# Reordering an encoder layer's expert stage: where the permutation is made, which experts come last, and what stands at the end

## The chip, the cores and the metric

The kernel runs on one core of a Trainium2 chip. The core has TensorE (PE, the matrix engine; its weight loads are listed apart as PEld), VectorE (DVE), ScalarE (ACT), GpSimd (POOL) and SyncE (SP), each with its own instruction queue, and 16 DMA engines that move data between the chip's memory (DRAM here) and the on-chip buffers (SBUF; PSUM receives what TensorE computes, in banks of 128x512 float32). The metric is the device time of one execution in microseconds (us).

## The reference

One layer of an encoder over 256 tokens of width 1024: a normalisation, three token mixers side by side, gates, an output projection, a second normalisation, and then a mixture of 32 experts with a last normalisation. The change touches only the last part:

```python
logits = xf @ w_router + b_router              # (256, 32)
top_val, top_idx = lax.top_k(logits, 4)        # four experts for each token
gates = softmax(top_val)
# for each expert e with its tokens:
u = x[toks] @ w1[e] + b1[e]                    # w1[e]: 1024 x 2048
glu, lin = split(u); glu = min(glu, 7); lin = clip(lin, -7, 7)
y = (glu * sigmoid(1.702 * glu) * (lin + 1)) @ w2[e] + b2[e]    # w2[e]: 1024 x 1024
out[toks] += y * gate
h = LN(alpha * h + out, ln2_g, ln2_b)          # alpha = 2 ** 0.25
```

Everything is float32. The weights of all 32 experts (12 MiB each, 384 MiB in all) are read once.

## The kernel before

The first 280 us or so (the trunk) compute the mixers, the second normalisation and the router. There the experts are ranked by their load; rank 0 is always expert 0, rank 1 is the most loaded of the others, rank 31 the least loaded. A rank has room for 128 tokens (ranks 0 to 5), 64 (6 to 19) or 32 (20 to 31). Ranks are put together to **units** of 128 token slots: one rank of 128, a pair of 64, or four of 32. `UNITS` is the order in which the 16 units run. The code behind it, under `tc.If(flag > 0)`, is a fallback for overfull experts; it reads `acc_out` and is skipped here.

**A unit.** `gather` picks the unit's tokens out of `h` with a 0/1 matrix `P` (made by `slots`), into `XT`. `up(u, side)` multiplies by w1: eight steps k, in each one 1 MiB block of w1 for each of the unit's ranks, four 128x512 products (into four `u` banks) for each rank. Products of a pair or of four ranks use 64 or 32 columns of the array each and run side by side. After each step, `used("w1", u, k)` gives the step's block buffers back, and `next(side)` records one piece of other work between this step's products and the next. When the loop is over, the sums are copied out, and the rest of `side` is recorded in one go (`for _ in side: pass`). `gated(u)` turns `U[u]` by TensorE transposes, adds the bias `b1` and computes the activation in two halves f. `down(u, side)` multiplies by w2 in four steps k, in each one 1 MiB block for each rank, with its own side work. `combine(u, t)` scatters a unit's result with `PC[u]` (made by `weigh`) and VectorE adds it to `acc_out`. The order is up(0), then up(u) and down(u-1) for u = 1 to 15, then `closing`, down(15) and `end`. `closing` starts four PSUM sums `acc` with `acc_out` and the last but one unit's result; `end` adds the last unit's, normalises, and stores.

**Side work before.** Beside up(0) stands `opening()`: the sorted list of ranks `pii`, which the loads of ranks 8 to 23 need (`ahead["all"]`), the token positions in rank order, the biases `b1` in rank order (16 small products and two copies by ScalarE), and gather(1). Beside up(1) stand gated(0), `gates()`, `begin` (which starts `acc_out`, with b2 read by a DMA on ScalarE's queue), weigh(0), weigh(1), slots(2), gather(2) and weigh(2). Beside down(14) stand gated(15) and `rows2`, which reads the last norm's gain and bias (`norms`) by a DMA on ScalarE's queue and spreads them over 128 partitions by eight small products.

**What sets the order.** From the trunk's last products on, PE, ACT, DVE and SP run in the order in which the code records them; nothing is rearranged. The weight blocks are read by SP (`pump`, L237) in the order of their use, except that w2 of unit 0 comes before w1 of unit 1. There are 19 buffers of 1 MiB (`RING`); one of them serves once, and the other 18 go round: a block can be read when the block that had its buffer has been used. A block's buffer is given back by the PE product that read it last.

**At the end.** `end` takes statistics of the four sums with VectorE, and works on one quarter with ScalarE and GpSimd, on the others with VectorE (`centre`, `spread`). `S.copy(acc_out[...], acc[...])` writes the four sums back for the fallback. `put` stores the quarters, four by SP and one by ScalarE's queue.

Of the kernel before, what the change touches and what calls it, by code (L numbers as in the profile page):

```python
# [23 lines left out]
T = 256  # L24
# [18 lines left out]


LARGE, MIDDLE = 5, 14
UNITS = [(0,), (28, 29, 30, 31), (1,), (6, 7), (2,), (8, 9), (20, 21, 22, 23), (3,), (10, 11), (4,), (12, 13),
         (24, 25, 26, 27), (5,), (14, 15), (16, 17), (18, 19)]
assert sorted(j for u in UNITS for j in u) == list(range(NE))


# [59 lines left out]
def encoder_layer(ctx, tc, consts, norms, columns, x, positions, w_in, w_gate, rel_bias, conv_w, w_pw2, w_uq, w_ukv,  # L110
# [20 lines left out]
    def bank(pool, name):  # L131
        return pool.tile([128, 512], F32, name=name)
# [853 lines left out]
    R = {}  # L986
# [100 lines left out]

    def opening():

        p = bank(pu, "m")  # L1090
        PE.matmul(p[:1, :NE], cst[:NE, C_P:C_P + 1], R["perm"][:NE], start=True, stop=True)
        R["pii"] = cp.tile([1, NE], I32, name="pii")
        V.tensor_copy(R["pii"], p[:1, :NE])
        ahead["all"] = True
        yield
        R["ps"] = (yield from transposed(R["posm"]))[1]
        slots(1)
        S.activation(cp.tile([128, 1], F32, name="junk"), ones[:, 0:1], AF.Sigmoid)
        yield
        R["b1"] = mp.tile([128, 16, NE], F32, name="b1")  # L1100
        for i in range(2):
            p = bank(pu, "m")
            r = slice(i * NE, (i + 1) * NE)
            for c in range(8):
                f = slice(c // 2 * 256 + c % 2, (c // 2 + 1) * 256, 2)
                PE.matmul(p[:, c * NE:(c + 1) * NE], R["b1r"][r, f], R["perm"][r], start=True, stop=True)

            S.activation(R["b1"][:, 8 * i:8 * i + 8], p[:, :8 * NE].rearrange("p (c e) -> p c e", c=8), AF.Identity,
                         bias=ones[:, 0:1] if i else 0.0)
            yield  # L1110
        yield from gather(1)

    def transposed(src):

# [112 lines left out]
    def up(u, side):  # L1227

        js = UNITS[u]
        n = 128 // len(js)  # L1230
        banks = {cb: pu.tile([128, 512], F32, name="u", bufs=4) for cb in (0, 2, 1, 3)}
        for k in range(8):
            for cb in (0, 2, 1, 3):
                for i, j in enumerate(js):
                    PE.matmul(banks[cb][i * n:(i + 1) * n], XT[u][:, k, i * n:(i + 1) * n],  # L1235
                              block["w1", j, k][:, 0, cb * 512:(cb + 1) * 512], start=(k == 0), stop=(k == 7),
                              skip_group_check=True)
            used("w1", u, k)
            next(side, None)
        us = U[u] = mp.tile([128, 2048], F32, name="us")  # L1240
        for cb, copy in ((0, S.copy), (2, V.tensor_copy), (1, S.copy), (3, V.tensor_copy)):
            copy(us[:, cb * 512:(cb + 1) * 512], banks[cb])  # L1242
        for _ in side:
            pass
# [48 lines left out]
    def beside_up(u):  # L1293

        if u == 1:
            yield
            yield from gated(0)
            yield from gates()
            for t in range(2):
                begin(t)  # L1300
                yield
            yield from weigh(0)
            yield from weigh(1)
        if u + 1 < n_units:
            slots(u + 1)
        yield
        for t in range(2):
            if u > 1:
                combine(u - 2, t)
                yield  # L1310
        if u + 1 < n_units:
            yield from gather(u + 1)
            yield from weigh(u + 1)

    def beside_down(u):

        yield
        if u + 1 < n_units:
            yield from gated(u + 1)
        if u + 2 == n_units:  # L1320
            yield from rows2()

    def experts():
        up(0, opening())
# [8 lines left out]

    def rows2():

        nf = mp.tile([128, T], F32, name="gp")[:8]
        nc.scalar.dma_start(out=nf, in_=norms[8:12].rearrange("r (i n) -> (r i) n", i=2))
        yield
        L["n"] = Norm(cp)
        v = R["slots"].rearrange("p (r i n) -> p r i n", r=4, i=2)  # L1340
        for r in range(4):
            p = bank(pu, "m").rearrange("p (i n) -> p i n", i=2)
            for i in range(2):
                PE.matmul(p[:, i], ident[:8, 2 * r + i:2 * r + i + 1].to_broadcast([8, 128]), nf, start=True, stop=True)
            S.copy(v[:, r], p)
        L["n"].gb = [[R["slots"][:, (2 * i + c) * 512:(2 * i + c + 1) * 512] for i in range(2)] for c in range(2)]
# [11 lines left out]
    def end(u):  # L1358
# [31 lines left out]
        V.tensor_scalar(n2.v[:, 0], n2.mv[:, :, 1], 1e-5, None, op0=OP.add)  # L1390
        centre(0, 1)
        rsqrt(n2.v[:, 1], n2.v[:, 0], n2.v[:, 2])
        for c in range(2):
            S.copy(acc_out[:, 0, cols(c)], acc[0, c])
        S.activation(o0, o0, AF.Copy, scale=n2.v[:, 1, 0:1])
        G_.tensor_add(o0, o0, n2.gb[0][1])
        for c in range(2):
            S.copy(acc_out[:, 1, cols(c)], acc[1, c])
        centre(1, 0)
        spread(0, 1)  # L1400
        centre(1, 1)
# [5 lines left out]
        put(1, 0)  # L1407
        for q in range(2):
            put(1, 1, slice(q * 256, q * 256 + 256))


    warm = tp.tile([128, 1], F32, name="warm")
# [237 lines left out]
```

## Time and profile before

| | |
|---|---|
| median of 3 runs | 1275.05 us (1273.71 to 1275.6) |
| profiled execution | 1275.57 us, of which the profile's span is 1273.7 us |
| PE busy | 1183.7 us, 93% of the span |
| VectorE, ScalarE, GpSimd busy | 412.5, 261.0 and 118.8 us |
| DMA | 449.35 MB, mean 353 GB/s |
| mean granted TensorE clock | 0.97 of full speed |

[...] A busy PE is not a PE at its peak: products are counted as busy for as long as they are in the pipeline, and those that run side by side count once. Each matrix product of float32 appears as two records in the trace, so a step of one rank, four products, is "x8", and a step of four ranks, 16 products, is "x32".

### The profile page before, as it was taken

How to read it: one execution, taken by the hardware profiler on the slowest of the kernel's cores; microseconds unless marked ns; L12 is line 12 of the kernel's file. 1: busy time of each engine (PE TensorE's matmuls, PEld its weight loads, DVE VectorE, ACT ScalarE, POOL GpSimd, SP SyncE). 2: the span in 40 equal slices, each digit the busy share in tenths (PEclk: the TensorE clock that was granted, in tenths of full speed). 3: DMA queues.
4: the chain of work that ended last, by engine and by line, in shares of the span. 5: the costliest groups of instructions: out<-in, count | busy, mean ns of one | idle time of the engine just before them, and what ended most of it. 6: DMA issues, size and time to landing. Idle time of an engine off the chain costs nothing.

```text
span 1273.7 us, 15502 instructions
## 1 busy us (share of the span) xinstructions
PE 1183.7 (93%) x6015; PEld 627.8 (49%) x6015; DVE 412.5 (32%) x705; ACT 261.0 (20%) x486; POOL 118.8 (9%) x164
## 2 busy tenths in 40 slices
PE   8998998999878999999979989999978989999786
PEld 6998988975315534534324424543322523434241
DVE  6568998850203131221202121221201221212012
ACT  5785785521101000010001000010100000100011
POOL 7441752002000000000000000000000000000000
PEclk9999999989988999999999999999998999999978
DMA  8636444599899799999999999999999999999970
GB/s 276 208 133 205 152 131 159 166 374 406 338 421 422 279 398 421 421 421 421 421 421 420 422 421 422 421 422 421 420 422 420 422 420 422 420 422 420 422 324 35
DMA packets 78727, 449.35 MB, mean 353 GB/s; under 512 B 7697, under 2 KB 9346, under 8 KB 29498
## 3 DMA queue, kind: packets, MB, share of 16 engines
q1 hardware_dynamic: 76266, 442.83, 86.2%
q0 software_dynamic: 1648, 4.15, 1.1%
q10 hardware_dynamic: 736, 1.34, 0.3%
q8 instruction: 49, 0.80, 0.3%
q14 instruction: 28, 0.23, 0.0%
HBM read 446.67 MB, written 1.09 MB: 352 GB/s over the span
## 4 chain that ended last, share of the span: by engine, by line
PE 53%; DMA 37%; DVE 8%; issue 1%; ACT 1%; SPq 0%; DVEq 0%; ACTq 0%
PE u L1235 21%; DMA more<-in_w_dram 15%; DMA hi<-in_w_dram 12%; PE y L1282 10%; PE mm L357 9%; DMA raw<-in_w_dram 5%; PE m L1180 4%; DMA klo<-in_w_dram 3%; DVE c L756 3%; PE mm L349 3%; DVE lo L274 2%; PE m L1223 2%; PE u L1259 1%; DMA lo<-in_w_dram 1%; DMA pts<-in_columns_dram 1%
## 5 line engine op out<-in xcount | busy, mean ns | idle before, releaser
L1235 PE MATMUL u<-more,xt 128*64 128x512 f32 (+2 forms) x840 | 246.9, 613 | 12.2 <-DMA more<-in_w_dram 12.1
L1235 PE MATMUL u<-lo,xt 128*32 128x512 f32 (+2 forms) x352 | 151.0, 624 | 4.6 <-DMA lo<-in_w_dram 4.6
L1235 PE MATMUL u<-hi,xt 128*32 128x512 f32 (+2 forms) x320 | 138.5, 621 | 11.2 <-DMA hi<-in_w_dram 11.2
L1235 PEld LDWEIGHTS u<-more,xt 128*64 128x64 f32 (+2 forms) x840 | 79.3, 142 | 130.6 <-issue 100.0
L1235 PE MATMUL u<-raw,xt 128*64 128x512 f32 (+2 forms) x304 | 129.4, 606 | 6.7 <-DMA raw<-in_w_dram 6.7
L1282 PE MATMUL y<-more,xt 128*32 128x512 f32 (+2 forms) x360 | 108.6, 615 | 3.6 <-DMA more<-in_w_dram 3.5
L1225 DVE TENSOR_TENSOR khi<-khi,m 128x512 f32<-128x512 f32 x56 | 38.5, 687 | 195.7 <-PE m L1223 195.7
L357 PE MATMUL mm<-klo,hi 128*128 128x256 f32 (+1 forms) x368 | 100.9, 286 | 0.0
L357 PE MATMUL mm<-khi,hi 128*128 128x256 f32 (+1 forms) x368 | 100.5, 285 | 0.1
L357 PE MATMUL mm<-khi,lo 128*128 128x256 f32 (+1 forms) x368 | 100.2, 285 | 0.0
L274 DVE TENSOR_TENSOR lo<-raw,hi 128x2048 fp32r<-128x2048 f32 (+3 forms) x46 | 86.4, 1892 | 25.1 <-ACT hi L269 25.1
L1372 POOL TENSOR_SCALAR minus<-ln_mv 128x1 f32<-128x1 f32 x1 | 0.2, 186 | 967.2 <-DVE ln_mv L1369 967.2
L1282 PE MATMUL y<-raw,xt 128*64 128x512 f32 (+2 forms) x200 | 85.9, 607 | 2.8 <-DMA raw<-in_w_dram 2.8
L1282 PE MATMUL y<-hi,xt 128*64 128x512 f32 (+2 forms) x184 | 83.2, 613 | 4.3 <-DMA hi<-in_w_dram 4.3
L1242 DVE COPY us<-u 128x512 f32<-128x512 f32 x32 | 21.9, 690 | 176.7 <-PE u L1235 176.7
L1282 PE MATMUL y<-lo,xt 128*64 128x512 f32 (+2 forms) x168 | 74.9, 605 | 1.8 <-DMA lo<-in_w_dram 1.8
L269 ACT CAST hi<-raw 128x2048 fp32r<-128x2048 f32 (+3 forms) x46 | 67.4, 1486 | 41.6 <-PE mm L357 24.3
L1235 PEld LDWEIGHTS u<-lo,xt 128*32 128x32 f32 (+2 forms) x352 | 41.3, 137 | 67.0 <-issue 55.4
L1180 PEld LDWEIGHTS m<-P,h 128*128 128x128 f32 x512 | 64.0, 201 | 20.4 <-issue 20.2
L357 PEld LDWEIGHTS mm<-khi,hi 128*128 128x128 f32 (+1 forms) x368 | 68.0, 190 | 1.7 <-issue 1.0
L357 PEld LDWEIGHTS mm<-klo,hi 128*128 128x128 f32 (+1 forms) x368 | 68.0, 190 | 0.6 <-issue 0.3
L357 PEld LDWEIGHTS mm<-khi,lo 128*128 128x128 f32 (+1 forms) x368 | 68.1, 190 | 0.2
(354 smaller groups left out, 1627.3 us busy)
## 6 DMA issues: line engine op xcount, KB each, us to landing
more<-in_w_dram SPq DMA_DIRECT2D x150, 1024.0 KB, 19.8
lo<-in_w_dram SPq DMA_DIRECT2D x65, 1024.0 KB, 19.8
raw<-in_w_dram SPq DMA_DIRECT2D x63, 1024.0 KB, 19.8
hi<-in_w_dram SPq DMA_DIRECT2D x63, 1024.0 KB, 19.8
klo<-in_w_dram SPq DMA_DIRECT2D x21, 1024.0 KB, 19.8
xt<-in_w_dram SPq DMA_DIRECT2D x21, 1024.0 KB, 19.8
raw<-in_w_gate_dram SPq DMA_DIRECT2D x12, 1024.0 KB, 5.3
raw<-in_w_in_dram SPq DMA_DIRECT2D x10, 1024.0 KB, 6.9
```

What stands on the lines that cost most here:

```text
L269: S.copy(a, r)
L274: V.tensor_sub(b, r, a.bitcast(F32))
L349: PE.matmul(st["b"][t], (xhi, xhi, xlo)[q][:, k0 + kk, r], w[:, kk] if fn is None else fn(w, kk), start=(k0 + kk == q == 0), stop=(k0 + kk ...
L357: PE.matmul(st["o"][i], f((whi, whi, wlo)[q], kk), (xhi, xlo, xhi)[q][:, k0 + kk], start=(k0 + kk == q == 0 and i % 2 == 0), stop=(k0 + kk ...
L756: V.scalar_tensor_tensor(acc[:, c], x_, w, acc[:, c], op0=OP.mult, op1=OP.add)
L1180: PE.matmul(p[:, kk], h[:, t, k * 128:(k + 1) * 128], P[u][:, t], start=(t == 0), stop=(t == 1))
L1223: PE.matmul(p, PC[u][:, t * 128:(t + 1) * 128], Y[u][:, cols(cb)], start=True, stop=True)
L1225: V.tensor_add(r, r, p)
L1235: PE.matmul(banks[cb][i * n:(i + 1) * n], XT[u][:, k, i * n:(i + 1) * n], block["w1", j, k][:, 0, cb * 512:(cb + 1) * 512], start=(k == 0) ...
L1242: copy(us[:, cb * 512:(cb + 1) * 512], banks[cb])
L1259: PE.transpose(ut[half][:, c * 128:(c + 1) * 128], U[u][:, at:at + 255:2], ident)
L1282: PE.matmul(y[cb][i * n:(i + 1) * n], A_[u][:, 2 * k + kk, i * n:(i + 1) * n], block["w2", j, k][:, kk, cols(cb)], start=(k == kk == 0), s ...
```

## The change

Five edits, all in the expert stage.

1. `pii`, the ranked biases and a preload of the Sigmoid table leave `opening()` for a new piece `ranked()`, which is the first side work of up(1). gather(1) thereby comes two steps earlier in up(0).
2. In up(1) alone, two pieces of side work are taken after each step, not one.
3. `UNITS`: the four ranks 24 to 27 move from place 11 to the end, and (4,) and (12, 13) change places.
4. The DMA of the last norm's rows is issued in the side work of up(15), and `rows2` is recorded after the first step of down(14), ahead of gated(15), in one piece.
5. The four copies to `acc_out` move behind the stores.

```diff
-         (24, 25, 26, 27), (5,), (14, 15), (16, 17), (18, 19)]
+         (14, 15), (5,), (16, 17), (18, 19), (24, 25, 26, 27)]
...
     def opening():
 
+        yield
+        R["ps"] = (yield from transposed(R["posm"]))[1]
+        slots(1)
+        yield
+        yield from gather(1)
+
+    def ranked():
+
         p = bank(pu, "m")
         PE.matmul(p[:1, :NE], cst[:NE, C_P:C_P + 1], R["perm"][:NE], start=True, stop=True)
         R["pii"] = cp.tile([1, NE], I32, name="pii")
         V.tensor_copy(R["pii"], p[:1, :NE])
         ahead["all"] = True
-        yield
-        R["ps"] = (yield from transposed(R["posm"]))[1]
-        slots(1)
         S.activation(cp.tile([128, 1], F32, name="junk"), ones[:, 0:1], AF.Sigmoid)
-        yield
         R["b1"] = mp.tile([128, 16, NE], F32, name="b1")
...
-        yield from gather(1)
...
-            next(side, None)
+            for _ in range(2 if u == 1 else 1):
+                next(side, None)
...
         if u == 1:
-            yield
+            yield from ranked()
             yield from gated(0)
...
+        else:
+            L["nf"] = mp.tile([128, T], F32, name="gp")[:8]
+            nc.scalar.dma_start(out=L["nf"], in_=norms[8:12].rearrange("r (i n) -> (r i) n", i=2))
...
     def beside_down(u):
 
-        yield
-        if u + 1 < n_units:
-            yield from gated(u + 1)
         if u + 2 == n_units:
-            yield from rows2()
+            rows2()
+        else:
+            yield
+        yield from gated(u + 1)
...
         rsqrt(n2.v[:, 1], n2.v[:, 0], n2.v[:, 2])
-        for c in range(2):
-            S.copy(acc_out[:, 0, cols(c)], acc[0, c])
         S.activation(o0, o0, AF.Copy, scale=n2.v[:, 1, 0:1])
         G_.tensor_add(o0, o0, n2.gb[0][1])
-        for c in range(2):
-            S.copy(acc_out[:, 1, cols(c)], acc[1, c])
...
+        for t in range(2):
+            for c in range(2):
+                S.copy(acc_out[:, t, cols(c)], acc[t, c])
```

In the rows below, which give the order of the instructions and no time, the target of a product stands before the arrow, and what it reads behind it; "x4" counts like products that follow each other. On PE in up(0), before (L1235 is w1, L1091 `pii`, L1118 and L1123 the positions, L1106 the biases, L1180 the gather):

```order
L1235 MATMUL u<-raw,xt 128x512 x4
L1091 MATMUL m<-lrow,cst 1x32
L1235 MATMUL u<-raw,xt 128x512 x4
L1118 MATMUL m<-cst,posm 32x128 x2
L1235 MATMUL u<-us,xt 128x512 x4
L1123 MATMUL m<-lrow,gp 128x32 x2
L1235 MATMUL u<-more,xt 128x512 x8
L1106 MATMUL m<-lrow,y 128x32 x8
L1235 MATMUL u<-more,xt 128x512 x4
L1106 MATMUL m<-lrow,y 128x32 x8
L1235 MATMUL u<-more,xt 128x512 x4
L1180 MATMUL m<-P,h 128x128 x8
```

and now (w1 is L1238, the positions L1121 and L1126, the gather L1183):

```order
L1238 MATMUL u<-raw,xt 128x512 x8
L1121 MATMUL m<-cst,posm 32x128 x2
L1238 MATMUL u<-us,xt 128x512 x4
L1126 MATMUL m<-lrow,gp 128x32 x2
L1238 MATMUL u<-more,xt 128x512 x8
L1183 MATMUL m<-P,h 128x128 x8
L1238 MATMUL u<-more,xt 128x512 x4
L1183 MATMUL m<-P,h 128x128 x8
L1238 MATMUL u<-more,xt 128x512 x8
```

`pii` and the 16 bias products have left; the two halves of the gather stand after the fifth and the sixth of the eight steps, not after the seventh and the eighth.

On PE between the last step of up(1) and down(0), before (L1216 is `begin`, L1203 `weigh`, L1180 the gather of unit 2, L1282 w2):

```order
L1235 MATMUL u<-lo,xt 32x512
L1235 MATMUL u<-hi,xt 32x512
L1216 MATMUL m<-y,gp 128x512 x4
L1203 MATMUL m<-cst,gp 128x128 x4
L1180 MATMUL m<-P,h 128x128 x16
L1203 MATMUL m<-cst,gp 128x128 x2
L1282 MATMUL y<-more,xt 128x512 x8
```

and now:

```order
L1238 MATMUL u<-lo,xt 32x512
L1238 MATMUL u<-hi,xt 32x512
L1183 MATMUL m<-P,h 128x128 x16
L1206 MATMUL m<-cst,gp 128x128 x2
L1286 MATMUL y<-more,xt 128x512 x8
```

`begin` and two of the three `weigh` now stand between the steps of up(1); the gather of unit 2 and its `weigh` are what is left behind the last step.

On PE at the end, before (L1259 is gated(15), L1282 w2 of unit 14 and, behind L1354, of unit 15; L1344 `rows2`, L1353 and L1354 `closing`):

```order
L1259 MATMUL u<-cst,us 128x128 x8
L1282 MATMUL y<-more,xt 64x512 x8
L1344 MATMUL m<-gp,cst 128x256 x8
L1353 MATMUL u<-khi,cst 128x512
L1354 MATMUL u<-y,pc 128x512
L1353 MATMUL u<-khi,cst 128x512
L1354 MATMUL u<-y,pc 128x512
L1353 MATMUL u<-khi,cst 128x512
L1354 MATMUL u<-y,pc 128x512
L1353 MATMUL u<-khi,cst 128x512
L1354 MATMUL u<-y,pc 128x512
L1282 MATMUL y<-more,xt 64x512 x8
```

and now, around `rows2` (L1349), which stands after the first step of down(14):

```order
L1286 MATMUL y<-lo,xt 64x512
L1286 MATMUL y<-hi,xt 64x512
L1349 MATMUL m<-gp,cst 128x256 x8
L1263 MATMUL u<-cst,us 128x128 x8
L1286 MATMUL y<-lo,xt 64x512
L1286 MATMUL y<-hi,xt 64x512
```

Three of four steps of down(14) have come between `rows2` and `closing`, and the products of unit 15 that follow `closing` are 16 a step for four ranks, 32 columns each.

## Rows read from the trace of the kernel before

**Rows 1.** The page: the span in 40 equal slices of 31.8 us, the GB/s that the DMA engines moved in each.

```profile
GB/s 276 208 133 205 152 131 159 166 374 406 338 421 422 279 398 421 421 421 421 421 421 420 422 421 422 421 422 421 420 422 420 422 420 422 420 422 420 422 324 35
```

**Rows 2.** The page: issues of weight blocks on SP's queue, KB of one, and the median us from issue to landing.

```profile
more<-in_w_dram SPq DMA_DIRECT2D x150, 1024.0 KB, 19.8
```

**Rows 3.** Busy time by stretch (from:to, length, each engine's busy us, granted clock, DMA share, GB/s): the stretches in which the weight stream runs below 421 GB/s.

```profile
422.00:454.00 32.00, 32.00 (x153) 15.29 (x152) 3.82 (x7) 2.13 (x4) 0.00 (x0) 1.00 0.72 255
315.00:330.00 15.00, 15.00 (x108) 7.52 (x107) 1.89 (x3) 1.76 (x3) 0.00 (x0) 1.00 0.64 234
```

**Rows 4.** The chain of waits from up(0) to down(0): start, us, what.

```profile
289.47 0.14 PE m L1091 x2
...
304.52 2.00 PE m L1106 x16
...
310.14 2.00 PE m L1106 x16
...
315.77 1.78 PE m L1180 x16
...
322.78 3.69 PE u L1235 x32
...
327.51 9.54 DMA lo<-in_w_dram
...
358.58 17.29 DMA hi<-in_w_dram
...
375.91 5.29 PE u L1235 x26
381.20 1.92 PE m L1216 x4
...
388.51 5.80 PE m L1180 x32
394.34 0.69 DVE xt L1182
...
395.51 0.41 PE m L1203 x2
```

**Rows 5.** VectorE in order of time in up(1): start, us, line, operation, and in brackets the idle time before it with what ended it.

```profile
330.56 0.69 DVE L1263 TENSOR_TENSOR g<-y,b 128x512 f32<-128x512 f32 x1 [5.87 <-PE y L1259]
...
333.17 0.69 DVE L1271 SCALAR_TENSOR_TENSOR xt<-y,l 128x512 f32<-128x512 f32 x1
...
338.41 0.16 DVE L1134 TENSOR_SCALAR nm<-m 128x2 f32<-128x2 f32 x1
...
340.17 0.59 DVE L1142 TENSOR_REDUCE G<-oh 128x64 f32<-128x256 f32 x1
```

**Rows 6.** Busy time by stretch: up(2) of one rank, down(1) of four, up(3) of a pair, down(2) of one.

```profile
411.55:446.25 34.70, 34.70 (x110) 17.16 (x113) 4.46 (x7) 2.72 (x5) 0.00 (x0) 1.00 0.77 291
446.25:462.70 16.45, 16.45 (x146) 5.92 (x148) 7.23 (x12) 1.79 (x3) 0.00 (x0) 1.00 0.96 375
462.70:499.20 36.50, 36.50 (x171) 13.91 (x171) 4.46 (x7) 2.72 (x5) 0.00 (x0) 1.00 1.01 421
499.20:515.05 15.85, 15.85 (x51) 8.21 (x50) 7.21 (x12) 1.79 (x3) 0.00 (x0) 1.00 1.01 422
```

**Rows 7.** The DMA view of 1205 to 1245 us in 40 slices of 1 us: GB/s.

```profile
GB/s 418 410 401 467 410 426 393 442 426 418 418 401 451 418 434 393 418 451 418 418 401 426 434 426 418 393 385 270 262 213 205 98 49 8 0 0 0 0 0 0
```

**Rows 8.** The chain of waits at the end.

```profile
1221.70 4.41 DMA gp<-in_norms_dram
...
1226.15 7.19 PE m L1344 x16
...
1243.47 13.88 PE y L1282 x64
1257.35 2.79 PE u L1364 x6
```

**Rows 9.** The same stretch in order of time, VectorE and ScalarE's queue.

```profile
1263.70 0.16 DVE L379 SCALAR_TENSOR_TENSOR ln_v<-ln_v 128x2 f32<-128x2 f32 x1
1265.19 0.75 DVE L1375 SCALAR_TENSOR_TENSOR us<-u,ln_mv,xt 128x512 f32<-128x512 f32 x1 [1.32 <-ACT khi L1398]
...
1268.74 0.38 ACTq L1384 DMA_DIRECT2D out_dram<-us  x1
```

**Rows 10.** Busy time by stretch at the end, during and after the wait for the norm's rows (the last three columns are granted clock, DMA share, GB/s).

```profile
1222.20:1226.10 3.90, 0.69 (x4) 0.00 (x0) 0.00 (x0) 1.17 (x2) 0.00 (x0) 0.96 1.01 418
1226.10:1239.30 13.20, 13.15 (x23) 7.67 (x24) 0.00 (x0) 2.34 (x4) 0.00 (x0) 0.50 0.65 268
```

**Rows 11.** Busy time by stretch of PE alone, in two units of four ranks that wait for their blocks: up(1) (the first row) and up(6).

```profile
345.00:347.50 2.50, 2.50 (x16) 0.54 1.02 367
...
655.00:657.50 2.50, 1.04 (x2) 1.00 1.02 423
657.50:660.00 2.50, 2.35 (x24) 1.00 1.02 426
```

**Rows 12.** The chain of waits: one step of down(1), four ranks, at full clock.

```profile
454.40 3.57 PE y L1282 x32
```

More of the change, by code (lines that the diff above doesn't have):

```diff
@@ L45 @@
 LARGE, MIDDLE = 5, 14
-UNITS = [(0,), (28, 29, 30, 31), (1,), (6, 7), (2,), (8, 9), (20, 21, 22, 23), (3,), (10, 11), (4,), (12, 13),
-         (24, 25, 26, 27), (5,), (14, 15), (16, 17), (18, 19)]
+UNITS = [(0,), (28, 29, 30, 31), (1,), (6, 7), (2,), (8, 9), (20, 21, 22, 23), (3,), (10, 11), (12, 13), (4,),
+         (14, 15), (5,), (16, 17), (18, 19), (24, 25, 26, 27)]
 assert sorted(j for u in UNITS for j in u) == list(range(NE))
@@ L1334, in rows2 @@
     def rows2():
-        nf = mp.tile([128, T], F32, name="gp")[:8]
-        nc.scalar.dma_start(out=nf, in_=norms[8:12].rearrange("r (i n) -> (r i) n", i=2))
-        yield
+        nf = L["nf"]
         L["n"] = Norm(cp)
```

## The prediction

> **What bounds the kernel now.** I read the page's slices first. From about 450 us to 1235 us the DMA engines move 420 to 422 GB/s without a break, whatever TensorE does [rows 1]: the stage is bound by the stream of weight blocks. A block of 1.049 MB takes 2.49 us at that rate, and an issue lands after 19.8 us, eight blocks' time, because eight are under way [rows 2]. So the end is the landing of the last block plus what follows it, and a change can gain in two ways only: by filling the places where the stream runs below its rate, or by shortening what follows.
>
> Then the stretches below the rate. 315 to 330 us ran at 234 GB/s, which is 15 x (1 - 234/421) = 6.7 us of stream lost; 422 to 454 us ran at 255 GB/s, 12.6 us lost [rows 3]. Both come from buffers given back too late. The chain says by whom: in the first, up(0) is PE work end to end, and the stream starts again when the first step of up(1) has run (322.78 + 3.69 = 326.5 us) [rows 4]; in the second, nothing is given back between the last step of up(1), which ends at 381.2, and the first of down(0), which starts at 395.9, while `begin`, `weigh` and the gather run alone [rows 4]. After that PE works without a pause and stays the one that is late.
>
> Last the end. The last bytes arrive between 1238 and 1239 us [rows 7]; I take 1238.5. But PE finishes its last w2 product only at 1243.47 + 13.88 = 1257.35 [rows 8], 18.85 us later, as it had stood for 4.4 us waiting for the norm's rows behind the weights in the queue and then ran 13 us at half clock [rows 8, 10]: all of down(15) lies behind the stream's end. From 1257.35 to the span's end are another 16.35 us.
>
> **The change, part by part.**
>
> *up(0).* Leaving: 0.14 + 2.00 + 2.00 = 4.14 us of PE [rows 4]. So up(1) starts 4.1 us earlier and its first step gives back four buffers at 322.4. The stream was idle then for lack of buffers, so it restarts 4.1 us earlier, and the block on which up(1) ends (its last step starts at 375.9 [rows 4]) lands at about 371.8. Nothing before that is late for it: `ranked` (4.1 us) comes behind the first step, the second step ends at about 330, and the four blocks given back first feed the stream until 332.4. The list `pii` is made later, but ranks 8 and 9 are first read by up(5).
>
> *up(1) with two pieces a step.* It removes what stood behind the last step: 395.92 - 381.20 = 14.72 us. What stays is the gather and one `weigh`. The gather's two halves cost 1.78 us each at full clock (as in up(0)) and 5.80 us together at half clock, as they did here after PE's pauses; `weigh` and its wait end 1.6 us behind the gather (394.3 to 395.9) [rows 4]. PE now comes from 5 us of products without a pause, so I take 3.56 + 1.6 = 5.2 us: 9.5 us less. Where do the removed pieces go? Between steps that wait for blocks. A step of four ranks needs four blocks, 9.95 us, and 3.57 us of PE [rows 12]. New waits arise there. Both halves of gated(0) are recorded together and use the same two banks, so the second waits until VectorE has read the first: 333.17 + 0.69 - 330.56 = 3.3 us from its first add to its last read [rows 5]. `gates` follows at once, and its transposes wait for the reduction, 340.76 - 338.41 = 2.4 us [rows 5]; queued behind both stand the next steps' products, and behind these the buffers. Added up: steps 1 to 7 are 25 us, `ranked` 4.1, gated(0) 2.4 + 2.7, `gates` about 4.5, `begin` 4.3, two `weigh` 1.8: 45 us from 318.6, so PE is ready for the last step at 363.6, 8 us before its blocks land. The third step ends at about 339 and the stream has blocks until 342: covered by 3 us; beyond these, every microsecond more is one of stream.
>
> So down(0) starts 4.1 + 9.5 = 13.7 us earlier. In the loss at 422 to 454 PE is the late one and the stream follows it, as long as there is loss left: the two stretches hold 6.7 + 12.6 = 19.3 us, more than 13.7. The stream ends 13.7 us earlier. Bounds: if the new waits use up the 4.1 and the gather runs at half clock, 14.72 - 5.8 - 1.6 = 7.3; at most 19.3.
>
> *The order of units.* A unit costs PE about 52 us whatever its ranks (34.7 + 16.45 and 36.5 + 15.85) [rows 6], but its blocks 29.9 us for one rank, 59.7 for a pair, 119 for four. Ranks of one and pairs now stand in a row of eight between the four-rank units, and PE falls behind. Counting from up(10,11), where PE has caught up, to the end of up(5): 88 blocks are used (16+4+16+8+8+8+16+4+8); PE takes 43 + 16 + 36.5 + 15.8 + 34.7 + 15.8 + 36.5 + 16 + 34.7 = 249 us, in which the stream brings 249/2.49 = 100. Twelve blocks wait unread, of 18 buffers: the stream still has five to fill and loses nothing. In the last unit PE catches up again (32 blocks, 80 us, against 36.5).
>
> What this buys is the end. w2 of the last unit is now 16 blocks, 40 us of stream, and `rows2`, gated(15) and `closing` fit before it: w2 of unit 14 has landed 40 us before the end, PE needs about 4 + 7 us for the rest. `rows2`'s DMA is issued in up(15), and 4.4 us [rows 8] are over long before down(14). Behind the last block stands one step of 16 products: 3.57 us at full clock [rows 12], 5.29 us if it starts at half, as in up(1) [rows 4], 7.1 if all of it does. I take 4.4, between the first two, so 18.85 - 4.4 = 14.4 us go. Bounds: 15.3, and 18.85 - 7.1 - 2.8 = 8.9, when the sums behind it (2.79 us [rows 8]) double too.
>
> *The copies.* VectorE's `centre` waited 1.32 us for ScalarE's copy of the same sums [rows 9]; it can start when the reciprocal chain ends at 1263.86, so the stores are 1.3 us earlier. The four copies follow the last store's issue, 2.3 us on ScalarE, beside the stores' landing. Should the end wait for ScalarE: its last instruction ends at 1269.1 now [rows 9] and would at 1267.8 + 2.3 = 1270.1, 1.0 us later. So 1.3, bounds -1.0 and 1.3.
>
> **Sum.** 13.7 + 14.4 + 1.3 = 29.4 us from the profiled execution's 1275.57 (its span and 1.87 us around it): 1246.2. The median of the runs is 0.5 below that execution: 1245.6. With the bounds: 7.3 + 8.9 - 1.0 = 15.2 (1259.9) and 19.3 + 15.3 + 1.3 = 35.9 (1239.2).
>
> **The rivals.**
>
> *The early part gives half.* The waits in up(1) use the cover of 3 us up, the gather runs cold: 7.3 for 13.7, so 1252. For it: PE's queue is in order, and 20 us of side work now stand before buffers. Against: 8 us of slack at the last step.
>
> *The clock.* In a four-rank unit PE does a piece at each landing and waits. In up(1) the clock was down to 0.54 when the fourth block of a step came; in up(6), with the same waits, it stayed at 1.00 [rows 11]. If it is down at the last landing and stays so: 7.1 for 4.4 and 2.8 for the sums, 5.5 us more, 1251. [...]
>
> *Slower: the buffers run out.* In the row of eight units the stream has five blocks, 12 us, left. If PE were later than that, it would starve, and a late microsecond would be one of time; to end slower than before PE must lose 12 + 29.4 = 41 us there, as it would if it ran that much of its work at half clock. At 50 us the time is 1245.6 + 38 = 1284. Against it: in units without waits the clock stood at 1.00 [rows 6], and PE has no reason to wait in this stretch.
>
> **How the numbers follow.** Forecast 0.72 (by itself 1241 to 1250), early half 0.13, clock 0.12, starved stream 0.03. The range 1239 to 1255 takes in the first three but for a mixture of the second and third near 1258. Two per mille, 2.6 us, is what can be told from no change. The first three cases are all faster: 0.97; of the last, 0.01 within and 0.02 slower.
>
> **What would show it.** Below-rate stretches at 315 to 330 shorter by 4 us, and at 422 to 454 nearly gone; down(0) starting near 382; 421 GB/s through the row of units, last bytes near 1225; no wait for the norm's rows; one step of 16 products between the last landing and the final sums; `centre` with no wait for ScalarE. It would be wrong if GB/s fell below 415 between 740 and 1110 us, or if PE stood still in up(1) while landed blocks lay unread and the stream paused.

## The result, and the profile after

The changed kernel takes 1246.28 us (median of 4 runs, 1245.27 to 1247.82) beside 1275.32 for the kernel before (4 runs, 1273.71 to 1276.79): ratio 0.9774 [0.9757, 0.9791]. Forecast were 1245.6 and a range of 1239 to 1255. Its profiled execution took 1245.27 with a span of 1243.4; before, 1275.57 with 1273.7. So 30.3 us have left the span; the sum said 29.4.

The page's GB/s in 40 slices, now of 31.1 us, answer to [rows 1]:

```profile
GB/s 287 205 140 178 178 136 126 181 325 421 386 412 421 410 408 421 421 421 421 421 421 421 421 421 421 421 421 421 422 420 422 421 421 422 421 420 421 421 422 134
```

The slice at 279 is gone, and from about 460 us to the last slice the stream stands at 420 to 422. Busy time by stretch, in the columns of [rows 3]:

```profile
315.00:330.00 15.00, 15.00 (x103) 6.86 (x105) 1.56 (x3) 3.51 (x6) 0.00 (x0) 0.89 0.93 354
422.00:454.00 32.00, 32.00 (x197) 11.92 (x197) 7.92 (x13) 3.92 (x7) 0.00 (x0) 1.00 0.98 397
...
460.00:1200.00 740.00, 710.00 (x3110) 292.06 (x3112) 148.93 (x241) 59.89 (x106) 0.00 (x0) 0.98 1.01 421
```

The first stretch now loses 15 x (1 - 354/421) = 2.4 us of stream (6.7 before), the second 32 x (1 - 397/421) = 1.8 (12.6 before): 15.1 us recovered. PE's timeline shows where the second came from. Columns are start, us, operation, and in brackets the idle time before it and what ended it:

```profile
371.85 0.62 PE L1238 MATMUL u<-hi,xt 128*32 128x512 f32 x1 [1.46 <-DMA hi<-in_w_dram]
...
375.40 3.84 PE L1183 MATMUL m<-P,h 128*128 128x128 f32 x32
380.44 0.41 PE L1206 MATMUL m<-cst,gp 128*128 128x128 f32 x2 [1.21 <-DVE gp L1202]
```

The last step of up(1) starts 4.1 us earlier than before (371.85, was 375.91) and ends at 375.40 in place of 381.20; behind it stand the gather at 3.84 us and one `weigh`, so down(0) starts at 380.85, not 395.92 [rows 4]. That is 15.1 us earlier, as much as the stream recovered.

The end, first by the DMA view of 1192 to 1232 us in 1 us slices, as [rows 7]:

```profile
GB/s 434 418 426 426 418 418 426 418 418 426 426 426 418 418 418 434 418 401 426 426 418 410 434 418 344 262 254 238 238 98 82 16 0 0 0 0 0 0 16 0
```

The last bytes of weights fall in 1223 to 1224 us, before in 1238 to 1239: 15.0 us earlier. PE and the other engines behind that, in order of time:

```profile
1224.42 0.62 PE L1286 MATMUL y<-more,xt 128*32 128x512 f32 x1 [1.41 <-DMA more<-in_w_dram]
...
1227.98 3.70 PE L1369 MATMUL u<-y,pc 128*128 128x512 f32 x8
...
1234.46 0.75 DVE L1380 SCALAR_TENSOR_TENSOR us<-u,ln_mv,xt 128x512 f32<-128x512 f32 x1
...
1238.36 0.38 ACTq L1389 DMA_DIRECT2D out_dram<-us  x1
1238.79 2.05 ACT L1413 COPY khi<-u 128x512 f32<-128x512 f32 x4 [3.42 <-DVEq L1561]
```

One step of 16 products (3.56 us) is all that is left between the last block and the final sums at 1227.98, where all of down(15) stood before. From the last bytes (1223.5, the middle of their slice) to the sums it is 4.5 us, from 18.85. `centre` (L1380) waits no longer, and the copies (L1413) run behind the last store's issue. From the final sums to the span's end it is 15.42 us, from 16.35.

15.0 + 14.4 + 0.9 = 30.3: the whole difference of the spans.

### The profile page after: what moved, and what is told of

The parts are those of the page before. It is cut to its first block, busy times and chain, and to the rows that moved or that the text cites. A ratio compares the mean times of both kernels' runs of the same rounds, so it can differ in the third digit from the quotient of the medians.

```text
span 1243.4 us, 15504 instructions
## 1 busy us (share of the span) xinstructions
PE 1167.6 (94%) x6015; PEld 615.8 (50%) x6015; DVE 414.2 (33%) x705; ACT 260.5 (21%) x486; POOL 118.7 (10%) x164
## 5 line engine op out<-in xcount | busy, mean ns | idle before, releaser
L1238 PE MATMUL u<-more,xt 128*64 128x512 f32 (+2 forms) x800 | 230.0, 621 | 9.8 <-DMA more<-in_w_dram 9.8
L1238 PE MATMUL u<-lo,xt 128*64 128x512 f32 (+2 forms) x376 | 165.6, 616 | 3.5 <-DMA lo<-in_w_dram 3.5
L1238 PE MATMUL u<-hi,xt 128*64 128x512 f32 (+2 forms) x352 | 155.9, 611 | 7.1 <-DMA hi<-in_w_dram 7.1
L1238 PE MATMUL u<-raw,xt 128*64 128x512 f32 (+2 forms) x288 | 128.5, 626 | 5.6 <-DMA raw<-in_w_dram 5.6
L1238 PEld LDWEIGHTS u<-more,xt 128*64 128x64 f32 (+2 forms) x800 | 73.3, 143 | 122.1 <-issue 96.5
L1286 PE MATMUL y<-more,xt 128*32 128x512 f32 (+2 forms) x400 | 125.5, 595 | 6.5 <-DMA more<-in_w_dram 6.5
L1286 PE MATMUL y<-raw,xt 128*64 128x512 f32 (+2 forms) x216 | 91.4, 599 | 1.4 <-DMA raw<-in_w_dram 1.4
L1238 PEld LDWEIGHTS u<-lo,xt 128*64 128x64 f32 (+2 forms) x376 | 46.1, 139 | 77.4 <-issue 67.8
L1286 PE MATMUL y<-hi,xt 128*64 128x512 f32 (+2 forms) x152 | 68.0, 608 | 5.6 <-DMA hi<-in_w_dram 5.6
L1183 PEld LDWEIGHTS m<-P,h 128*128 128x128 f32 x512 | 62.0, 196 | 21.0 <-issue 21.0
L1286 PEld LDWEIGHTS y<-more,xt 128*32 128x32 f32 (+2 forms) x400 | 42.6, 142 | 55.8 <-issue 40.2
## 6 DMA issues: line engine op xcount, KB each, us to landing
xt<-in_w_dram SPq DMA_DIRECT2D x21, 1024.0 KB, 19.8
```

The lines of the kernel that those rows point to most:

```text
L1183: PE.matmul(p[:, kk], h[:, t, k * 128:(k + 1) * 128], P[u][:, t], start=(t == 0), stop=(t == 1))
L1286: PE.matmul(y[cb][i * n:(i + 1) * n], A_[u][:, 2 * k + kk, i * n:(i + 1) * n], block["w2", j, k][:, kk, cols(cb)], start=(k == kk == 0), s ...
```

## The experiments

Each edit is against the kernel named. Ratios are to the kernel before, run beside it.

**The end: the order of units, the norm's rows, or both?**

*1. The order alone.* Before, with the new order of units.

```diff
-         (24, 25, 26, 27), (5,), (14, 15), (16, 17), (18, 19)]
+         (14, 15), (5,), (16, 17), (18, 19), (24, 25, 26, 27)]
```

> The kernel before with only the new order of units (four ranks 24 to 27 last). Theory (the end is the stream's end plus what PE still has to do): the stream still ends near 1238.5 us; rows2, though at its old place behind the norm's DMA, falls into the 30 us in which PE waits for the last unit's blocks, so its 4.4 us wait and the half clock cost nothing; one step of 16 products is left. Gain 14 us, 1261. Rival (the wait for the norm's rows and the slow clock behind it are what the old end cost, the order of units is secondary): gain at most 5 us, 1270.

Measured: 1276.36 us, ratio 1.0014 [0.9995, 1.0033]. No gain: the theory's 1261 fell. The rival's bound, a gain of at most 5 us, held, and what it names, the wait for the norm's rows, is what the trace shows. The chain of waits at the end:

```profile
1202.69 19.78 DMA more<-in_w_dram
1222.49 4.49 DMA gp<-in_norms_dram
1227.02 7.19 PE m L1344 x16
...
1242.70 13.87 PE y L1282 x128
```

and PE's timeline at the third of these:

```profile
1227.02 7.19 PE L1344 MATMUL m<-gp,cst 8*128 8x256 f32 x16 [23.23 <-DMA gp<-in_norms_dram]
```

PE stands for 23.23 us, with the stream at 422 and 423 GB/s over 1200 to 1220 us, because `rows2` heads its queue and waits for 8 KB of norm. That DMA starts as a certain weight block lands, 0.02 us after it. The built program's list of instructions says why (of before: the first row on ScalarE's queue, the others on SP's, the eighth and the seventh weight block from the end):

```
363 L1337 DMA gp<-in_norms_dram 8x256 [waits DMAHW5_49]
856 L237 DMA more<-in_w_dram 128x2048 [waits DMAHW5_49,PE_49]
858 L237 DMA more<-in_w_dram 128x2048 [waits DMAHW6_49,PE_49]
```

In this program the DMAs of both queues share eight completion counters, DMAHW0 to DMAHW7, in turn: of the 461 in the list, the skipped fallback's included, each counter has 57 or 58. The norm's DMA has to wait until the DMA before it on counter 5 has landed, and that is the eighth weight block from the end. Before has the same link: a block issued at 1201.92 lands at 1221.69, the norm's DMA begins at 1221.70 [rows 8].

*2. The rows alone.* Before, with edit 4.

```diff
+        else:
+            L["nf"] = mp.tile([128, T], F32, name="gp")[:8]
+            nc.scalar.dma_start(out=L["nf"], in_=norms[8:12].rearrange("r (i n) -> (r i) n", i=2))
...
     def beside_down(u):
-        yield
-        if u + 1 < n_units:
-            yield from gated(u + 1)
         if u + 2 == n_units:
-            yield from rows2()
+            rows2()
+        else:
+            yield
+        yield from gated(u + 1)
```

> The kernel before with only the norm's rows moved (DMA in up(15), rows2 after the first step of down(14)), old order of units. Theory: PE no longer waits 4.4 us, keeps full clock in closing (7 us) and down(15) (14 us), and ends its last w2 product near 1245 and not 1257: gain 12 us, 1263; so the two edits are substitutes, each taking nearly the same time away. Rival (the edits add up): what the order alone leaves of the 14 us.

Measured: 1266.94 us, ratio 0.9928 [0.991, 0.9947]: 8.6 us of the 12 expected, and with experiment 1 at nothing the two edits are no substitutes. The chain at the end:

```profile
1205.92 3.65 PE y L1282 x14
1209.56 3.72 PE m L1345 x16
1213.28 1.92 PE u L1259 x8
...
1234.79 13.88 PE y L1282 x64
1248.67 2.79 PE u L1365 x6
```

The final sums stand at 1248.67, 8.7 us earlier than 1257.35 [rows 8]. How long PE itself stood in before, its own timeline says; the 4.41 us of [rows 8] are the DMA's time, and PE was still at work for the first part of them:

```profile
1226.15 7.19 PE L1344 MATMUL m<-gp,cst 8*128 8x256 f32 x16 [3.26 <-DMA gp<-in_norms_dram]
```

This wait of 3.26 us has left. `rows2` (L1345) takes 3.72 us from 7.19, and `closing`, which ran partly at half clock behind that wait (granted 0.50 from 1226.1 to 1239.3 us [rows 10]), 7.07 from 10.12: together 9.8 us. A wait of 1.33 us for a block of down(14) has left as well. Against these stand the products of gated(15) behind `rows2`, 1.92 us from 1.15, and a start of down(14) that is 1.6 us later in this execution (1205.92, 1204.32 before). All of down(15) still lies behind the stream.

*3. The changed kernel with the old order.* The diff of experiment 1, the other way round.

> The changed kernel with the old order of units. Theory: all of down(15) of a pair (14 us) lies behind the stream's last blocks again, but without the norm's wait: 2 us slower than the changed kernel, 1248. Rival (the order carries the end): 10 us or more slower, 1256.

Measured: 1250.24 us, ratio 0.9804 [0.9762, 0.9846], 4 us more than the changed kernel, between the theory's 2 and the rival's 10; the intervals of the ratios overlap, so the trace has to carry it. Its PE timeline:

```profile
1229.14 3.60 PE L1286 MATMUL y<-more,xt 128*64 128x512 f32 x16
```

The last step begins with no wait at 1229.14 and the final sums at 1232.67, 4.7 us later than in the changed kernel, though the last bytes have come by 1224 here too. PE is still behind when the stream ends. That is what the order is worth once the norm's rows are out of the way: about 4.7 us.

*4. The changed kernel with the norm's DMA and rows at their old place.* Edit 4 undone.

> The changed kernel with the norm's DMA and rows2 at their old place behind down(14)'s side work. Theory: hidden in the wait for the last unit's blocks, 0 to 1 us slower, 1246 to 1247. Rival (the wait for the norm's rows carries the end): 8 us or more slower, 1254.

Measured: 1259.12 us, ratio 0.9869 [0.9826, 0.9912]: 13 us more than the changed kernel, and the theory's number fell. PE's timeline, and ScalarE's queue:

```profile
1213.39 7.19 PE L1348 MATMUL m<-gp,cst 8*128 8x256 f32 x16 [23.34 <-DMA gp<-in_norms_dram]
```

```profile
1208.75 0.52 ACTq L1341 DMA_DIRECT2D gp<-in_norms_dram  x1
```

The wait of experiment 1 is back, 23.34 us, and the final sums come at 1243.87, 15.9 us later than in the changed kernel; the two profiled executions lie 15.8 us apart. In the changed kernel the same 8 KB are issued in up(15):

```profile
1109.47 0.52 ACTq L1320 DMA_DIRECT2D gp<-in_norms_dram  x1
```

*5. The DMA early, the products late.* The changed kernel with the DMA in up(15), but `rows2` behind gated(15).

```diff
     def beside_down(u):
+        yield
+        yield from gated(u + 1)
         if u + 2 == n_units:
             rows2()
-        else:
-            yield
-        yield from gated(u + 1)
```

> The changed kernel with the norm's DMA where the change puts it (up(15)), but rows2's eight products at their old place behind down(14)'s last step. Theory, formed on the runs before this one (the norm's DMA shares eight completion counters with the weight blocks, and at its old place it has to wait for the eighth block from the end of the stream): only the DMA's place matters; the products fall into PE's wait for the last unit: 1246 to 1247, as the changed kernel. Rival (the place of the products matters, since they stand before closing): 1259, as with all of rows2 at its old place.

Measured: 1248.03 us (1244.84 to 1249.06), ratio 0.9781 [0.9759, 0.9804], the profiled span 1243.0: the changed kernel within what the runs can tell. Of edit 4 it is the DMA's place that counts, not the products'.

**The early part.**

*6. Two pieces a step alone.* Before, with edit 2.

```diff
-            next(side, None)
+            for _ in range(2 if u == 1 else 1):
+                next(side, None)
```

> The kernel before with only the two pieces of side work a step in up(1). Theory: the stream's first gap (315 to 330 us) stays, the block on which up(1) ends lands at 375.9 as before, but 11 us less stand between it and down(0): the second gap (422 to 454 us, 12.6 us) all but closes. Gain 11 us, 1264. Rival (the side work only moves into waits that then delay the buffers in up(1)): gain under 5 us.

Measured: 1267.48 us, ratio 0.9924 [0.9898, 0.995]: 8.3 us, of 11 expected.

```profile
315.00:330.00 15.00, 15.00 (x92) 8.45 (x94) 2.28 (x4) 1.88 (x4) 0.00 (x0) 1.00 0.66 247
422.00:454.00 32.00, 32.00 (x189) 15.20 (x191) 6.39 (x11) 2.82 (x6) 0.00 (x0) 1.00 0.91 358
```

*7. The changed kernel with one piece a step.* That line back.

> The changed kernel with one piece of side work a step in up(1), as before; the ranking and biases stay beside up(1). Theory: the 4 us won in up(0) are half lost again, since one more piece (half of begin) stands behind the last step: down(0) starts near 394, 13 us later than in the changed kernel: 1259. Rival (the move out of up(0) is most of the early gain): 1252 or less.

Measured: 1257.02 us, ratio 0.9846 [0.9823, 0.9869], 10.7 us more than the changed kernel.

```profile
315.00:330.00 15.00, 15.00 (x114) 7.19 (x116) 1.56 (x3) 3.52 (x6) 0.00 (x0) 1.00 0.90 345
400.00:422.00 22.00, 22.00 (x62) 10.53 (x61) 8.60 (x14) 2.38 (x4) 0.00 (x0) 1.00 0.93 370
422.00:454.00 32.00, 32.00 (x175) 15.02 (x177) 6.17 (x10) 2.73 (x5) 0.00 (x0) 1.00 0.72 270
```

The two experiments cross. With edit 2 alone the first gap stays (247 GB/s, 234 before) and the second mostly closes (358, 255 before); without it, but with edit 1, the first closes (345) and the second stays (270). So edit 1 answers for the first gap and edit 2 for most of the second. But without edit 2 the second gap also begins earlier: 400 to 422 us runs at 370 GB/s, where the kernel before has 421. Of the 4.0 us that edit 1 wins in the first gap 1.6 are lost again in the second. By stretches, before loses 19.3 us, experiment 6 loses 11.0, experiment 7 loses 2.7 + 2.7 + 11.5 = 16.9, and the changed kernel 4.2: edit 2 recovers 8.3 us by itself, edit 1 only 2.4 without edit 2, and the two together 15.1. Edit 1 alone was not run; experiment 7 stands for it in these stretches, since its other edits act later.

*11. Nothing left behind the last step.* The changed kernel with three pieces a step from the fifth step on.

```diff
-            for _ in range(2 if u == 1 else 1):
+            for _ in range((3 if k > 3 else 2) if u == 1 else 1):
```

> The changed kernel with three pieces of side work a step from the fifth step of up(1) on, so that the gather of unit 2 and its weigh stand before the last step's products too. Theory: PE stands ready 6 us before the last step's blocks land, so the 4 us gather is free there, and down(0) starts 5 us earlier; but the second gap holds only about 2 us of stream still lost, and no more can be won: 2 us faster, 1244.3. Rival (5 us earlier is 5 us less): 1241. Other rival (the side work delays the buffers): slower.

Measured: 1245.01 us (1244.79 to 1247.87), ratio 0.978 [0.9757, 0.9804]. PE, the stretch, and SP's last issue:

```profile
365.46 3.84 PE L1183 MATMUL m<-P,h 128*128 128x128 f32 x32
```

```profile
422.00:454.00 32.00, 32.00 (x202) 11.25 (x203) 9.29 (x15) 3.54 (x6) 0.00 (x0) 1.00 1.01 420
```

```profile
1202.25 2.82 SPq L237 DMA_DIRECT2D more<-in_w_dram  x2
```

The gather now runs before the last step, and the stretch is whole at 420 GB/s. Yet the last blocks are issued at 1202.25, as in the changed kernel (1202.24), and its span is the same, 1243.4: in the trace the 2 us expected are not there. Where they went, the DMA view of 1195 to 1235 us shows, in 1 us slices:

```profile
GB/s 401 459 401 442 401 426 434 418 418 401 451 410 434 410 393 442 401 434 401 352 254 262 238 238 188 82 25 33 16 0 0 0 0 0 0 16 0 0 0 16
```

The rate leaves its level at 1214 us, two slices earlier than in the changed kernel (344 at 1216), and the last bytes come in the same slice, 1223 to 1224. From 352 on, this ending moves in ten slices what takes 4.0 us at 421 GB/s: 6.0 us are lost. In the changed kernel it is 8 - 3.6 = 4.4. So 1.6 of the 1.8 us recovered at 422 to 454 are given back at the stream's end. The mean rate here told when most bytes were through, and not when the last block landed. The DMA engines' mean busy share falls with the rate (0.6 and 0.5 over 1215 to 1219 us); why is not shown, as no view has the 16 one by one.

**The row of units: how much room has the stream?**

*8. A little more PE work.* The changed kernel with matmuls whose result nobody reads, two products in each up of seven units from up(10,11) on (28 matmuls in the trace, 0.59 us each as recorded, 0.43 us apart where products follow each other), 12 us in all.

```diff
+    def extra(n):
+        p = bank(pu, "m")
+        for _ in range(n):
+            PE.matmul(p, ident, acc_out[:, 0, 0:512], start=True, stop=True)
...
             used("w1", u, k)
+            if 8 <= u <= 14 and k % 4 == 3:
+                extra(1)
```

> The changed kernel with two more 128x512 products on PE (1.7 us) in each up of the seven units from place 8 to 14, which leaves the result as it is: 12 us of PE in all, 8.6 of them before the end of up(5). Theory as predicted (the stream has five blocks, 12 us, left there): no cost, 1246 to 1247. Rival (the margin is smaller than that count, because buffers come back a step at a time and PE's lag peaks inside a unit): most of the 12 us shows, about 8: 1254.

Measured: 1251.0 us, ratio 0.9795 [0.977, 0.982]; the span is 1249.3, 5.9 us longer. The theory's "no cost" fell.

```profile
980.00:1000.00 20.00, 20.00 (x75) 8.64 (x74) 2.41 (x4) 1.54 (x3) 0.00 (x0) 1.00 0.92 363
1060.00:1100.00 40.00, 40.00 (x180) 15.43 (x178) 7.17 (x12) 3.58 (x7) 0.00 (x0) 1.00 0.99 391
```

Two stretches fall below the rate: 20 x (1 - 363/421) = 2.8 and 40 x (1 - 391/421) = 2.9, together 5.7 us. That looks like the whole 5.9, and isn't. PE's timeline at the end:

```profile
1227.33 1.06 PE L1294 MATMUL y<-more,xt 128*32 128x512 f32 x1 [1.37 <-DMA more<-in_w_dram]
...
1233.86 3.70 PE L1377 MATMUL u<-y,pc 128*128 128x512 f32 x8
```

The last step starts only 2.9 us later than in the changed kernel (1224.42), and then takes 6.53 us in place of 3.56: the granted clock is 0.53 over 1227.3 to 1233.8 us and the first product takes 1.06 us; over the same step of the changed kernel they are 1.00 and 0.62 us. That is the other 3.0 us. And the stream makes up for the rest of its 5.7 at its end, here from 1195 to 1235 us:

```profile
GB/s 410 434 410 418 434 418 418 410 442 418 434 418 401 418 426 410 410 434 426 426 418 426 426 418 418 410 434 418 426 328 156 33 0 0 0 0 0 0 0 0
```

The rate falls to nothing within three slices, where the changed kernel takes eight: 1.8 us are lost in this ending, 4.4 there. So some 9 of the 12 us added were covered.

*12. Four times as much.* The same with `k % 2 == 1: extra(2)`, 48 us in all.

> The changed kernel with eight more 128x512 products on PE (6.9 us) in each up of the seven units from place 8 to 14, which leaves the result as it is: 48 us in all. Theory (once the buffers are full a late microsecond of PE is one of stream): at the margin of 12 us as predicted 36 us are lost, 1282; at the margin that the smaller dose shows, 7 us, 41 us, 1287: slower than the kernel before. Rival (PE's extra work falls into its waits in the four-rank units): under 20 us.

Measured: 1283.04 us, ratio 1.0078 [1.0053, 1.0103]: slower than the kernel before.

```profile
850.00:1170.00 320.00, 320.00 (x1302) 135.61 (x1302) 67.42 (x109) 24.90 (x44) 0.00 (x0) 1.00 0.92 369
```

The changed kernel has 421 GB/s in this stretch. 320 x (1 - 369/421) = 39.5 us of stream are lost, and the span is 37.1 longer; the last step starts 37.1 us later and takes 3.55 us, so here all of it is the stream's. Some 11 of the 48 us were covered, close to the margin of 12 that gave the theory's 1282.

**The copies.**

*9. The copies back at their place.* The changed kernel with edit 5 undone.

> The changed kernel with the four copies to acc_out at their old place ahead of the stores. Theory: VectorE's centre waits 1.3 us for them again, and 0.4 us of what the change loses in VectorE's last operations beside GpSimd comes back: 1 us slower, 1247.3. Rival (the chain in the changed kernel ends with the copies, so they now set the end): no slower, or 1 us faster.

Measured: 1247.53 us, ratio 0.9799 [0.9774, 0.9824]: the times can't tell it from the changed kernel. VectorE in order of time:

```profile
1237.25 0.75 DVE L1380 SCALAR_TENSOR_TENSOR us<-u,ln_mv,xt 128x512 f32<-128x512 f32 x1 [1.32 <-ACT khi L1403]
```

The wait of 1.32 us [rows 9] is back, and from the final sums to the span's end it is 16.36 us, not 15.42. The whole times differ by more than the copies: in this execution the last step starts 1.6 us earlier than in the changed kernel and runs at half clock (granted 0.54), 6.48 us for 3.56:

```profile
1222.86 1.06 PE L1286 MATMUL y<-more,xt 128*32 128x512 f32 x1 [1.42 <-DMA more<-in_w_dram]
...
1229.34 3.70 PE L1369 MATMUL u<-y,pc 128*128 128x512 f32 x8
```

*10. No copies at all.* The changed kernel without them.

```diff
-        for t in range(2):
-            for c in range(2):
-                S.copy(acc_out[:, t, cols(c)], acc[t, c])
```

> The changed kernel without the four copies; acc_out, which only the skipped fallback reads, is then not written back. Theory: they run beside the landing of the stores and cost nothing: 1246.3, within 0.5 us. Rival (they end the chain): 2 us faster, 1244.

Measured: 1246.48 us, ratio 0.9786 [0.9761, 0.9811]; from the final sums to the end 15.43 us. The changed kernel's page gives the chain that ended last as nothing but these copies:

```profile
ACT khi L1413 0%; ACTq L1389 0%; ACTq L1560 0%
```

They are last in time and cost nothing: without them the end comes 15.43 us after the sums, with them 15.42.

## Why the prediction was right, and where its reasons were not

*up(0)* held. Buffers are given back at 322.03 (forecast 322.4):

```profile
322.03 0.33 SPq L237 DMA_DIRECT2D lo<-in_w_dram  x1
```

and the block on which up(1) ends lands at 371.85 (371.8).

*up(1)* held in its mechanism and was a little small in size. The new waits that were feared are there:

```profile
332.93 0.74 PE L1263 MATMUL y<-cst,us 128*128 128x128 f32 x4 [0.97 <-DVE l L1267]
334.94 0.74 PE L1263 MATMUL y<-cst,us 128*128 128x128 f32 x4 [1.27 <-DVE xt L1275]
```

They add to 2.2 us. PE stands ready for the last step at 365.80, 2.2 us later than the 363.6 worked out and still 6 us before its last block, so the rival "the early part gives half" fell. The sum missed that the last step of up(1) would run at full clock as well: 3.55 us at a granted clock of 1.00, not 5.29 at 0.68. That is 1.7 of the difference between 15.1 us and the 13.7 forecast; the gather with its `weigh`, at 5.45 and not 5.2, takes 0.25 back (granted 1.00 there; before, the gather took its 5.80 us at 0.62).

*The end* came out in size (14.4 us forecast, 14.4 found) and was wrong in its reason. The prediction wrote that the order of units buys the end, and that PE had "stood for 4.4 us waiting for the norm's rows behind the weights in the queue", a small wait that the change would merely hide. PE stood for 3.26 us (experiment 2), and the order alone buys nothing (experiment 1). The norm's DMA, tied to the landing of a late block by its counter, would have held PE for 23 us in the new order. In before, a pair as last unit leaves only eight blocks behind the w2 of unit 14, and PE was busy with that w2 until nearly the moment when the DMA came, so only the rest of the wait showed. Taking the norm's rows forward gives 8.7 us alone (experiment 2) and 13 in the company of the new order (experiment 4), and the order some 4 to 5 on top of it (experiment 3): neither part earns the end alone. The forecast was safe only because the change holds both. That the size came out to a tenth is luck as well: the last step took 3.56 us, not 4.4, and the 0.9 us from the last bytes (1223.5) to that step's start (1224.42) stood in no term of the sum.

*The clock* as a rival did not come up in the profiled execution: the last step, after a wait of 1.41 us, took 3.56 us at full clock. That too is luck. Behind the same kind of wait (1.37 and 1.42 us) the same step took 6.53 us in experiment 8 and 6.48 in experiment 9, at a granted clock of 0.53 and 0.54, and 5.25 in experiment 7, at 0.68. Five of the eight profiled executions with this end ran it in 3.55 or 3.56 us. So the rival's first half, up to 7.1 us for the step, does happen; its second, the sums behind it doubled, does not: from them to the end it is 15.43 us in experiment 8, and 15.42 in the changed kernel. In up(15) of the changed kernel, with waits for blocks again, a burst ran at a lower clock as well:

```profile
1164.92 5.34 PE L1238 MATMUL u<-more,xt 128*32 128x512 f32 x26 [0.58 <-DMA more<-in_w_dram]
```

The granted clock is 0.66 over 1160 to 1170 us, and 1.00 over 1190 to 1228.5, where down(15) waits. So a burst between waits for blocks ran at a lower clock in up(15), and in down(15) of experiments 7, 8 and 9, and not in down(15) of the changed kernel. What decides between them no run here shows.

*The row of units* lost nothing, as forecast, and the room in it, "five blocks, 12 us", was put a little high: by the start of the last step some 9 of 12 us were covered in experiment 8, and 11 of 48 in experiment 12. Counting bytes lost by the mean rate instead would have made it 6 and 8.5. The slower rival's mechanism is real (experiment 12): 48 us more of PE work end 9 us behind the kernel before, so some 39 would have been even, where the prediction had 41. Nothing in the changed kernel costs that much.

*The copies*: 0.9 us, forecast 1.3. The wait did go; the difference is in the last section.

## What to carry to other kernels

Before an 8 KB DMA is put down as hidden, look up which DMA it has to follow on its completion counter: here, next to a stream with eight blocks under way, it began 0.02 us after a block that took 19.8 us to land, PE stood 23.23 and 23.34 us for it in experiments 1 and 4, and the profile of the kernel before shows only the 3.26 us that no other work covered. The order that puts less work behind the last transfer paid here only once nothing at the head of PE's queue was tied to a late one (ratio 1.0014 alone, some 4 to 5 us once the norm's rows had moved). A chain that ends last in time may cost nothing, as the copies here (15.43 us from the sums to the end without them, 15.42 with them), so take its work out once before trusting it. A sum of stretches below the stream's rate can be off by some us from the landing of the last block (5.7 us lost in experiment 8, and a last step 2.9 us later), and a difference of spans can hide a step that ran at another clock (6.53 us at 0.53, 3.56 at 1.00): look up both before two numbers that agree are taken for cause and effect.

## What was not expected of the hardware

VectorE's multiplication by the reciprocal (`spread`, L1385) became slower when the copies moved, at a moment when it now runs beside GpSimd's addition for longer. Groups of the changed kernel over the end, with busy us and mean ns of one, and idle time before:

```profile
L1385 DVE SCALAR_TENSOR_TENSOR us<-us,ln_v,xt 128x512 f32<-128x512 f32 x2 | 1.8, 919 | 0.0
...
L1399 POOL TENSOR_TENSOR us<-us,xt 128x512 f32<-128x512 f32 x1 | 1.6, 1552 | 1.3 <-ACT us L1398 1.3
```

and of the kernel before:

```profile
L1380 DVE SCALAR_TENSOR_TENSOR us<-us,ln_v,xt 128x512 f32<-128x512 f32 x2 | 1.5, 740 | 0.0
...
L1396 POOL TENSOR_TENSOR us<-us,xt 128x512 f32<-128x512 f32 x1 | 1.3, 1267 | 1.3 <-ACT us L1395 1.3
```

919 ns for 740, and 1552 for 1267 on GpSimd; with the copies back (experiment 9) VectorE's is at 744 again. Without any copies (experiment 10) the three `spread` that stand last take 1.89 us together, as in the changed kernel, so it is the moment that counts and not the copies. In order of time in the changed kernel:

```profile
1235.13 0.74 DVE L1385 SCALAR_TENSOR_TENSOR us<-us,ln_v,xt 128x512 f32<-128x512 f32 x1
...
1236.45 1.89 DVE L1385 SCALAR_TENSOR_TENSOR us<-us,ln_v,xt 128x512 f32<-128x512 f32 x3
```

```profile
1235.44 1.55 POOL L1399 TENSOR_TENSOR us<-us,xt 128x512 f32<-128x512 f32 x1 [1.30 <-ACT us L1398]
```

The first began before GpSimd's addition and took its 0.74 us; the second began at 1236.45, while the addition ran (to 1236.99), and took 2 x 0.919 - 0.74 = 1.10. These 0.36 us are about what the copies' gain lacks of 1.3. The addition, begun 0.43 us before the first one's end (1235.87), took 1.55 us, 0.28 more than before. In the kernel before the two ran side by side for 0.17 us only, the addition from 1264.76 to 1266.03 and the first `spread` from 1265.86, and that `spread` took 0.74 us. Why both take longer in the changed kernel no view here shows.
